# Row sums of the later modulation: four products, or a weighted sum on VectorE and one product

## The chip, the cores and the metric

The kernel runs on one core of a Trainium2 chip. The metric is the device time of one execution in microseconds (us). Before the change it is 3398.08 us, the median of 3 runs (3396.28 to 3401.31).

## What is computed

The reference is one layer of a decoder trunk for 1,024 tokens of width 2,048. Two sub-layers (a token mixer with four head groups, and a mixture of experts) are each modulated by shift, scale and gate vectors. All six vectors come from one product of the conditioning vector c with a matrix of 2,048 rows and 12,288 columns:

```python
mod = (jax.nn.silu(c) @ w_ada[l] + b_ada[l]).astype(F32)
sh1, sc1, gt1, sh2, sc2, gt2 = jnp.split(mod, 6, axis=-1)
h = ada_input(x, sh1, sc1)
p = h @ w_in[l]
...
x = layer_norm(ALPHA * x + (1.0 + gt1)[:, None, :] * y_mix, ln_g[l, 0], ln_b[l, 0])
h = ada_input(x, sh2, sc2)
```

The change touches only how the last four of these vectors (gt1, sh2, sc2, gt2: 8,192 columns) are computed.

## The kernel before

**Stages.** Up to about 55 us the kernel normalizes tokens and begins the first two vectors. From there to about 2,000 us it runs the input projection, the four mixers and the output projection; then routing and the experts follow, to the end at about 3,400 us.

**The order on TensorE.** In the middle stage two streams share TensorE. The mixers (RWKV, attention, S5) are written out by hand; their products depend on VectorE and ScalarE. The fills are the projections: `fills` runs over units of columns, and `unit` over 16 row tiles, with three products per tile pair (`mm3`). Wherever a mixer would wait, it calls `hop(us)`, and `pump` takes fills until their estimated cost covers that time: 0.64 for each `mm3`, 0.9 for each modulation step (`modstep`, line 618). In this stage every TensorE instruction is kept in the order of the program text (`pinned`, line 191). The other engines' orders, and that of the DMA queue on SyncE (SP), are set by the compiler's scheduler.

**Weights of the fills.** A row tile is loaded to `wraw` (four buffers), rounded by ScalarE to `whi` (line 327), and the rest is taken by VectorE to `wlo` (line 328); there are three buffers of each pair.

**The modulation steps.** `mod_parts` (line 577) is a generator with 64 steps: 16 groups `ci` of 512 columns, and in each four steps `q` of four row tiles. It is advanced once for every four row tiles of a unit (line 397). A step takes four tiles of 128 rows and 512 columns, loaded by line 587 into `mw` buffers, of which there are six (`mt`, line 221); `conv` (line 919) takes three of the same six each time. For each tile `w` four products follow (line 601), one for each 128 columns: the stationary operand is the column of silu(c) for that row tile, repeated over 32 columns, and the output is a strip of 32 partitions of `pq`, a part of the PSUM tile `rwS`. The four tiles accumulate in `pq`. After the first step of a group VectorE copies `pq` to `mdacc` (line 605), after the next two it adds (line 607), and in the last (q = 3) the bias row is added by a product with a row of ones (line 603), VectorE makes the sum (line 610), and four small DMAs write it out. Then the loads of the next step are issued (line 615). The trace counts each f32 product as two records, so a step is 32 records of weight loads and 32 of products, and the bias is 8 of each.

**The triangular solve.** `rw_core` (line 720) has a loop of 31 steps in which VectorE multiplies and reduces (lines 788 and 789); its result goes to DRAM and comes back before the next mixer products, 32 by 32 in shape (line 822).

Of the kernel before, what the change touches and what calls it, by code (L numbers as in the profile page):

```python
# [15 lines left out]
ALU = mybir.AluOpType  # L16
# [7 lines left out]
KT = D // 128  # L24
# [144 lines left out]
class K:  # L169
# [407 lines left out]
    def mod_parts(s):  # L577


        nc, io = s.nc, s.io  # L580
        jobs = [(ci, q) for ci in range(KT) for q in range(4)]

        def load(ci, q):
            ws = []
            for k in range(4 * q, 4 * q + 4):
                ws.append(s.mt())
                nc.sync.dma_start(ws[-1], io["w_ada"][128 * (KT * ci + k):128 * (KT * ci + k) + 128])
            if q == 3:
                ws.append(s.ev())
                nc.sync.dma_start(ws[-1][0:1], io["b_ada"][0:1, 2 * D + 512 * ci:2 * D + 512 * ci + 512])  # L590
            return ws

        ws = load(*jobs[0])
        yield
        pq, pm = s.rwS[:, 128:256], s.mdacc
        for i, (ci, q) in enumerate(jobs):
            for x, w in enumerate(ws):
                k = 4 * q + x
                for j in range(4):
                    if k < KT:  # L600
                        s.mm(pq[32 * j:32 * j + 32], s.cs[:, k:k + 1].to_broadcast([128, 32]), w[:, 128 * j:128 * j + 128], start=x == 0, stop=x == 3 and q < 3)
                    else:
                        s.mm(pq[32 * j:32 * j + 32], s.c["ones"][0:1, 0:32], w[0:1, 128 * j:128 * j + 128], start=False, stop=True)
            if q == 0:
                nc.vector.tensor_copy(pm, pq)
            elif q < 3:
                nc.vector.tensor_add(pm, pm, pq)
            else:
                t = ws[4][:, 0:128]
                nc.vector.scalar_tensor_tensor(t, pm, 0.0 if ci // 4 == 1 else 1.0, pq, op0=ALU.add, op1=ALU.add)  # L610
                for j in range(4):
                    nc.sync.dma_start(s.md_d[0:1, 512 * ci + 128 * j:512 * ci + 128 * j + 128], t[32 * j:32 * j + 1])
                s.nmd += 1
            if i + 1 < len(jobs):
                ws = load(*jobs[i + 1])
            yield
# [1625 lines left out]
```

## Time and profile before

| | us |
|---|---|
| median of 3 runs | 3398.08 |
| the profiled execution | 3401.34 |
| its span, first to last instruction | 3399.5 |
| TensorE products busy | 2914.0 (86%) |
| TensorE weight loads busy | 2198.7 (65%) |
| VectorE busy | 1879.4 (55%) |
| ScalarE busy | 1157.6 (34%) |

The profile page gives busy time by engine, a strip of 40 slices of about 85 us, the DMA queues, and the costliest groups of instructions. PE is TensorE's products, PEld its weight loads, DVE VectorE, ACT ScalarE, POOL GpSimd, SPq the DMA queue of SyncE. The trace can also be asked for groups of instructions by form, for who waited for whom, for busy time in windows, and for instructions in order of time. "Idle before" is the time an engine stood still just before the instructions of a group; behind "<-" stands what ended it, and "issue" means that nothing the profile shows was waited for.

### The profile page before, as it was taken

The numbers are of one execution on the slowest core, as the hardware profiler recorded it, in microseconds if no ns is written. First come the engines' busy times: TensorE is split into PE (matmuls) and PEld (weight loads), VectorE is DVE, ScalarE is ACT, GpSimd is POOL, SyncE is SP. The second block draws the span as 40 slices with busy tenths as digits, with TensorE's granted clock in tenths as the row PEclk, the third lists the DMA queues.
The fourth block names the chain that finished last, engine by engine and source line by source line (L and its number), as shares of the span: only waits on it lengthen the run. The fifth ranks groups of instructions, "written<-read, shape, count | busy, mean of one in ns | idle before, by whom it ended". The sixth has DMA issues, their size and how long they took to land. (4 is left out here: it accounts for less than half of the span.)

```text
span 3399.5 us, 58570 instructions
## 1 busy us (share of the span) xinstructions
PE 2914.0 (86%) x22607; PEld 2198.7 (65%) x22607; DVE 1879.4 (55%) x3504; ACT 1157.6 (34%) x1808; POOL 544.6 (16%) x678
## 2 busy tenths in 40 slices
PE   6889989899999999989998865798897988988950
PEld 3567666766687667667677754676665766766740
DVE  2466667774443465666646883255454454454527
ACT  4332323333322322332433441234343343343411
POOL 0057665200000000000004452000001010010002
PEclk9999999999999999999998876898998988989975
DMA  8646354654798667445347666989899799799884
GB/s 352 220 150 180 105 166 126 210 170 150 249 302 271 215 194 224 124 132 162 100 140 239 211 219 250 383 317 401 326 342 385 295 385 381 286 395 364 310 324 198
DMA packets 348842, 845.96 MB, mean 249 GB/s; under 512 B 95505, under 2 KB 175482, under 8 KB 284770
## 3 DMA queue, kind: packets, MB, share of 16 engines
q1 hardware_dynamic: 338812, 808.36, 66.2%
q0 software_dynamic: 9728, 33.61, 3.8%
q8 instruction: 184, 3.01, 0.4%
q14 instruction: 118, 0.97, 0.1%
HBM read 752.35 MB, written 108.87 MB: 253 GB/s over the span
## 5 line engine op out<-in xcount | busy, mean ns | idle before, releaser
L1893 DVE TENSOR_TENSOR partl<-raw,parth 128x1024 fp32r<-128x1024 f32 x336 | 405.3, 1222 | 319.6 <-ACT parth L1892 313.8
L328 DVE TENSOR_TENSOR wlo<-wraw,whi 128x512 fp32r<-128x512 f32 (+2 forms) x472 | 355.4, 756 | 365.4 <-ACT whi L327 352.8
L327 ACT CAST whi<-wraw 128x512 fp32r<-128x512 f32 (+2 forms) x472 | 282.4, 601 | 736.1 <-PE acc L182 590.7
L1892 ACT CAST parth<-raw 128x1024 fp32r<-128x1024 f32 x336 | 347.9, 1050 | 455.4 <-PE h L182 188.9
L182 PE MATMUL acc<-hh,whi 128*128 128x512 f32 (+1 forms) x1056 | 456.4, 437 | 11.8 <-ACT hh L354 6.4
L182 PE MATMUL acc<-hh,wlo 128*128 128x512 f32 (+1 forms) x1056 | 421.8, 401 | 21.4 <-DVE wlo L328 21.3
L182 PE MATMUL acc<-hl,whi 128*128 128x512 f32 (+1 forms) x1056 | 421.9, 400 | 0.0
L182 PE MATMUL acc<-wlo,hh 128*128 128x512 f32 x640 | 263.1, 411 | 23.1 <-DVE wlo L328 20.2
L182 PE MATMUL acc<-whi,hh 128*128 128x512 f32 x640 | 264.2, 432 | 21.7 <-DVE ev L1534 16.0
L182 PE MATMUL h<-partl,xh 128*128 128x512 f32 x608 | 259.0, 426 | 17.3 <-DVE partl L1893 17.1
L182 PE MATMUL h<-parth,xh 128*128 128x512 f32 x608 | 243.0, 420 | 24.9 <-ACT parth L1892 24.5
L182 PEld LDWEIGHTS acc<-hh,whi 128*128 128x128 f32 (+1 forms) x1056 | 203.2, 193 | 87.6 <-issue 33.1
L182 PE MATMUL acc<-whi,hl 128*128 128x512 f32 x640 | 259.5, 405 | 0.0
L182 PEld LDWEIGHTS acc<-hh,wlo 128*128 128x128 f32 (+1 forms) x1056 | 201.9, 191 | 73.5 <-DVE wlo L328 26.2
L182 PE MATMUL h<-parth,xl 128*128 128x512 f32 x608 | 248.4, 408 | 0.0
L182 PEld LDWEIGHTS acc<-hl,whi 128*128 128x128 f32 (+1 forms) x1056 | 202.6, 192 | 46.8 <-issue 10.2
L182 PE MATMUL h<-raw,x 128*32 128x128 f32 x4608 | 169.2, 286 | 25.5 <-DMA raw<-in_moe_w 21.8
L1564 POOL MEMSET pre<- 128x516 int32 x1 | 0.5, 527 | 1084.5 <-DMA r_d<-ev 1084.5
L182 PEld LDWEIGHTS h<-raw,x 128*32 128x32 f32 x4608 | 130.8, 114 | 64.3 <-issue 33.6
L182 PEld LDWEIGHTS acc<-whi,hh 128*128 128x128 f32 x640 | 124.8, 197 | 66.0 <-issue 16.9
L182 PEld LDWEIGHTS acc<-wlo,hh 128*128 128x128 f32 x640 | 126.1, 197 | 56.9 <-DVE wlo L328 28.3
L182 PEld LDWEIGHTS h<-partl,xh 128*128 128x128 f32 x608 | 121.0, 199 | 64.3 <-DVE partl L1893 31.9
(448 smaller groups left out, 4761.3 us busy)
## 6 DMA issues: line engine op xcount, KB each, us to landing
raw<-in_moe_w SPq DMA_DIRECT2D x384, 1024.0 KB
mw<-in_w_ada SPq DMA_DIRECT2D x256, 256.0 KB
wraw<-in_w_in SPq DMA_DIRECT2D x240, 256.0 KB
wraw<-in_w_out SPq DMA_DIRECT2D x160, 256.0 KB
wa<-in_wa SPq DMA_DIRECT2D x32, 1024.0 KB
pT_d<-ev SPq DMA_DIRECT2D x62, 256.0 KB
t<-s_tab SPq DMA_DIRECT2D x24, 512.0 KB
s_tab<-mw SPq DMA_DIRECT2D x32, 256.0 KB
```

Of the source, the lines that this page charges most:

```text
L182: return s.pinned(s.nc.tensor.matmul(*a, **k))
L327: s.nc.scalar.copy(v(hi), v(raw))
L328: s.nc.vector.tensor_sub(v(lo), v(raw), v(hi).bitcast(F32))
L1564: nc.gpsimd.memset(pre.bitcast(I32), BIG)
L1892: nc.scalar.copy(hi, x)
L1893: nc.vector.tensor_sub(lo, x, hi.bitcast(F32))
```

## The change

In the steps with odd q (1 and 3), VectorE multiplies the first tile by its column of silu(c), in place, and adds the three other tiles, each times its column. Four products of a matrix of ones (128 by 32) with that tile follow, one for each strip of 128 columns. The steps with even q stay as they are, as do the bias products, the sums in `mdacc`, the loads and the pacing value of 0.9.

```diff
@@ -594,8 +594,18 @@
         yield
         pq, pm = s.rwS[:, 128:256], s.mdacc
         for i, (ci, q) in enumerate(jobs):
+            if q % 2:
+
+                a = ws[0]
+                nc.vector.tensor_scalar(a, a, s.cs[:, 4 * q:4 * q + 1], None, op0=ALU.mult)
+                for x in range(1, 4):
+                    nc.vector.scalar_tensor_tensor(a, ws[x], s.cs[:, 4 * q + x:4 * q + x + 1], a, op0=ALU.mult, op1=ALU.add)
+                for j in range(4):
+                    s.mm(pq[32 * j:32 * j + 32], s.c["ones"][:, 0:32], a[:, 128 * j:128 * j + 128], start=True, stop=q < 3)
             for x, w in enumerate(ws):
                 k = 4 * q + x
+                if q % 2 and k < KT:
+                    continue
                 for j in range(4):
                     if k < KT:
                         s.mm(pq[32 * j:32 * j + 32], s.cs[:, k:k + 1].to_broadcast([128, 32]), w[:, 128 * j:128 * j + 128], start=x == 0, stop=x == 3 and q < 3)
```

## Rows read from the trace of the kernel before

**Rows 1.** TensorE's busy tenths in 40 slices; the steps' products, first and last start

```profile
PE   6889989899999999989998865798897988988950
...
L182 PE MATMUL rwS<-mw,cs x2048: 272/273/418, 704.1 to 1363.9; 128*32 128x128 f32 x187
```

**Rows 2.** Busy time of 704 to 1365 us (columns as the first line says)

```profile
core 0: us, PE busy (x) PEld busy (x) DVE busy (x) ACT busy (x) POOL busy (x), PEclk, DMA share, GB/s
704.00:1365.00 661.00, 639.01 (x5281) 468.62 (x5282) 340.56 (x790) 202.37 (x381) 0.10 (x1) 0.98 0.71 227
```

**Rows 3.** PE's waits, 704 to 1365 us, longest first: total, times, longest

```profile
PE rwA L182 <- ACT t L1037: 3.9, 1, 3.9
PE rwS L182 <- DMA mw<-in_w_ada: 3.8, 7, 1.3
```

**Rows 4.** Groups by form: products of the steps and of the bias

```profile
L182 PE MATMUL rwS<-mw,cs 128*32 128x128 f32 x2048 | 71.1, 276 | 4.4 <-DMA mw<-in_w_ada 3.8 <-DVE St L876 0.6
...
L182 PE MATMUL rwS<-ev,per 1*32 1x128 f32 x128 | 6.7, 280 | 0.0
```

**Rows 5.** Weight loads in order of time at a q = 3 step: start, duration

```profile
943.21 0.81 PEld L182 LDWEIGHTS rwS<-mw,cs 128*32 128x32 f32 x32
944.22 0.15 PEld L182 LDWEIGHTS rwS<-ev,per 1*32 1x32 f32 x8 [0.20 <-issue]
944.57 0.19 PEld L182 LDWEIGHTS acc<-hh,whi 128*128 128x128 f32 x1 [0.20 <-issue]
944.68 0.19 PEld L182 LDWEIGHTS acc<-hl,whi 128*128 128x128 f32 x1
944.91 0.19 PEld L182 LDWEIGHTS acc<-hh,wlo 128*128 128x128 f32 x1
```

**Rows 6.** VectorE in `conv`: shortest, median and longest duration in ns

```profile
L930 DVE TENSOR_SCALAR mw<-mw,vecs x8: 478/481/487, 550.0 to 1467.9; 128x512 f32<-128x512 f32 x8
...
L931 DVE SCALAR_TENSOR_TENSOR mw<-mw,vecs x8: 732/747/754, 551.6 to 1468.6; 128x512 f32<-128x512 f32 x8
```

**Rows 7.** The page's groups: the rounding of the fills' weights

```profile
L328 DVE TENSOR_TENSOR wlo<-wraw,whi 128x512 fp32r<-128x512 f32 (+2 forms) x472 | 355.4, 756 | 365.4 <-ACT whi L327 352.8
L327 ACT CAST whi<-wraw 128x512 fp32r<-128x512 f32 (+2 forms) x472 | 282.4, 601 | 736.1 <-PE acc L182 590.7
```

**Rows 8.** Two solves in order of time: VectorE's last reduction, then TensorE's next products

```profile
1222.26 0.42 DVE L789 TENSOR_REDUCE t<-tv 128x8 f32<-128x256 f32 x1
...
1239.99 0.69 PE L182 MATMUL rwB<-t,t 32*32 32x32 f32 x32
...
1476.73 0.42 DVE L789 TENSOR_REDUCE t<-tv 128x8 f32<-128x256 f32 x1
...
1486.58 0.90 PE L182 MATMUL rwB<-t,t 32*32 32x32 f32 x32 [4.22 <-DMA t<-xn_d]
```

**Rows 9.** Loads of tiles and the products that waited for them, in time

```profile
1235.01 0.81 SPq L587 DMA_DIRECT2D mw<-in_w_ada  x2
...
1239.39 0.42 PE L182 MATMUL rwS<-mw,cs 128*32 128x128 f32 x8 [0.35 <-DMA mw<-in_w_ada]
...
1312.85 0.33 SPq L587 DMA_DIRECT2D mw<-in_w_ada  x1
...
1315.71 0.42 PE L182 MATMUL rwS<-mw,cs 128*32 128x128 f32 x8 [0.32 <-DMA mw<-in_w_ada]
...
1330.41 0.42 PE L182 MATMUL rwS<-mw,cs 128*32 128x128 f32 x8 [0.50 <-DMA mw<-in_w_ada]
```

**Rows 10.** Waits of SP's queue and of ACT, 680 to 1370 us

```profile
SPq L587 <- PE rwS L182: 79.1, 79, 5.7
...
ACT t L1265 <- DMA t<-u_d: 23.3, 7, 4.6
```

**Rows 11.** Busy time of two short windows (columns as in rows 2)

```profile
1350.30:1353.70 3.40, 1.59 (x31) 0.70 (x30) 0.69 (x1) 0.62 (x1) 0.00 (x0) 1.00 0.85 226
1353.70:1357.10 3.40, 3.40 (x15) 2.44 (x16) 0.29 (x1) 0.00 (x0) 0.00 (x0) 0.51 0.94 285
```

## The prediction

> **What bounds the kernel now.** I read the strip of 40 slices first, to see which engine is full where the modulation steps run. The steps' products start between 704.1 and 1363.9 us, slices 9 to 16, and TensorE stands there at 9 tenths in nearly every slice [rows 1]. Next the busy time of that stretch: of 661 us TensorE's products cover 639.0, its weight loads 468.6, VectorE 340.6 (52%), ScalarE 202.4, GpSimd nothing, and the granted clock is 0.98 of full [rows 2]. A modelled busy time doesn't prove a bound, so the list of waits comes third: of what TensorE's products wait for in this stretch, the longest total is 3.9 us, in one wait, and the second is 3.8 us for the tiles `mw` of the steps themselves [rows 3]. VectorE, in turn, stands idle mostly for ScalarE's rounding, which stands idle for TensorE to free its buffers [rows 7]. So the other engines wait for TensorE, and here TensorE's own work is the time. What it saves in this stretch should shorten the kernel, since the later stages follow from the fills in order.
>
> **What is removed from TensorE.** A step is 32 records. In order of time, the weight loads of a q = 3 step begin at 943.21, those of the bias at 944.22, those of the next fill at 944.57 [rows 5]. So 32 records take 1.01 us up to the next instruction, and 8 take 0.35, with a fixed 0.20 of turnaround in both. An odd step goes from 32 records to 8 of nearly the form of the bias products: it saves 1.01 - 0.35 = 0.66 us. There are 32 odd steps of 64, so 32 x 0.66 = 21.1 us. The ends: the bare loads go from 0.81 to a quarter, 0.20, which gives 32 x 0.61 = 19.5; the groups' busy times, 71.1/64 = 1.11 and 6.7/16 = 0.42 [rows 4], give 32 x 0.69 = 22.1. I take 21.1, from the starts, since they are what the next instruction sees.
>
> **What is added to VectorE.** One multiplication by a column and three multiply-adds, each 128 by 512 in f32 from SBUF. `conv` has both in the same form: 0.481 and 0.747 us [rows 6]. A step costs 0.481 + 3 x 0.747 = 2.72 us, all 32 cost 87 us. VectorE goes from 340.6 to 428 of 661 us (65%). I cost this at nothing by itself, for two covers. First, the weights of the fills: a product of a fill starts every 0.23 us (944.68 to 944.91, [rows 5]), a pair of buffers serves 12 products, 2.8 us, and two pairs are in hand when the third is refilled: 5.5 us, less 0.60 of rounding and 0.76 of subtraction [rows 7], leaves 4.2 us, more than 2.72. Second, the mixers' own chains, which the list of waits shows to be late for little [rows 3]. If the first cover is gone, each odd step costs what goes beyond 4.2 us.
>
> The tightest chain is the triangular solve, a loop of VectorE alone: one ends at 1222.68, and TensorE takes up its result at 1239.99 without a wait, 17.3 us later. Another ends at 1477.15, and there TensorE has to wait until 1486.58, so the way through DRAM takes 9.4 us [rows 8]. The slack of the first is 17.3 - 9.4 = 7.9 us. In a unit of two column tiles a step comes after every 24 products of 0.23 us, so with its own 1.01 us they stand 6.5 us apart; the solve's 31 hops of 0.88 us cover some 28 us of fills, so two of the four steps in it are odd. With one that begins before, two or three sums fall into it, 5.4 to 8.2 us, and TensorE comes 1.3 to 2.0 us earlier: the stall is between 0 and 2.3 us. I take 1.1 us, the middle, for this one solve, and nothing for others in the stretch, which could cost as much each at the upper end.
>
> **The wait that is added.** The four products now wait for VectorE, which waits for all four tiles. Behind the products stands everything on TensorE; behind the sums stand the next `wlo` and the mixers. The loads are issued a step ahead. Two tiles were in buffers before, and the last two are issued when the step before has freed theirs. From such an issue to the products that waited for it I read 4.4 us (1235.01 to 1239.39) and 2.9 us (1312.85 to 1315.71) [rows 9]. After the last tile TensorE had only its own records to do; now up to two multiply-adds come between, 1.5 us. Most odd steps hide this: their last loads are issued about 1 us into the step before, 5.5 us or more ahead, against 3.7 us of landing (the mean of the two) and 1.5. The three that waited for a tile before, at 1239, 1315 and 1330 [rows 9], pay it: 3 x 1.5 = 4.5 us. The ends are a gain of 3.8 us, where the waits for tiles go altogether because VectorE frees three buffers of an odd step before TensorE comes to it, and a loss of 1.5 us in each of ten odd steps, 15 us.
>
> SP's queue holds the loads until TensorE frees a buffer: 79 waits, 79.1 us [rows 10]. After an odd step it waits for VectorE instead, which is earlier, and the weights of the fills queued behind come no later. The number and size of all DMAs stays. The copies and sums in `mdacc`, the bias products and the pacing value of 0.9 stay, at nothing.
>
> A wait can also cost clock. Between 1350.3 and 1353.7 TensorE waited for tiles, with weight loads busy for 0.70 of 3.40 us; in the next window the granted clock was 0.51, the 1.2 GHz level, after 1.00 before [rows 11]. A window of 3.4 us at half the clock is worth up to 1.7 us. The Trainium skill, "TensorE: Matmul & The Clock Gate", section "HAM oscillation", says that repeated waits between short bursts make every burst start at the lower clock, which would speak against a change that adds waits. By that rule the three waiting steps would cost up to 3 x 1.7 = 5 us more, and the sum would come out 5 us higher. The row agrees in kind. I leave it out of the sum, since the stretch as a whole ran at 0.98 [rows 2], and keep it for the range.
>
> **Sum.** -21.1 + 4.5 + 1.1 = -15.5 us against the profiled execution's own 3401.34, which gives 3385.8. That execution is 3.3 us above the median of 3398.08; against the median the sum is 3382.6. I say 3383. By the ends of the terms it lies from -22.1 - 3.8 (3372) to -19.5 + 4.5 + 2.3 + 5 (3390); further losses belong to the rivals.
>
> **Rivals.** What a measurement of this kernel can tell from no change is about 0.2%, 6.8 us: 3391.3 to 3404.9 counts as the same.
>
> *The time saved is waited away.* An odd step still reports 0.9 to the pacing but takes 0.66 us less, so each mixer product that stands behind it comes 0.66 us sooner and, where its operand was just in time, waits that much longer. For it: the weight loads cover only 71% of the stretch [rows 2], so TensorE may have less to gain than its products' 97% says. Against it: the mixers' operands are late in few places now [rows 3], while the same TensorE saving is made in front of all the fills. The Trainium skill, "Perfetto Trace Analysis", section "Identifying the Most-Contended Engine", says that busy matmul time is a poor measure and that of the weight loads a good one; by it TensorE isn't full here, and the time would stay at 3398. The waits in this trace don't agree so far. This decides where the added waits reach 0.66 us for each odd step; ten steps at 1.5 us and 2.3 at the solve leave -4 us, 3394, and all of it gives 3398. Together with the case that the sum is right in sign but falls short of 6.8 us, this has a chance of 0.25.
>
> *VectorE is held at the head of its queue (slower).* Its order is fixed beforehand. Where a sum was put in front of work that is ready, but its tile lands late, everything behind it waits: `wlo`, then TensorE. For it: ScalarE is held that way now, 7 times by the load of `u_d`, for 3.3 us on average and 4.6 at most [rows 10], and tiles take 2.9 to 4.4 us to land. Against it: half of a step's tiles are there long before. Price: a hold of 3.3 and 2.72 of work, less the cover of 4.2, is 1.8 us for each odd step, 58 in all; less 21 that is +37, 3435. It decides where the hold exceeds 4.2 - 2.72 + 0.66 = 2.1 us; at 2.5 us it is +11, 3409. Chance 0.20.
>
> That the change doesn't do what it says can be left out: the removed products are skipped in the program text.
>
> **How the numbers follow.** The forecast's case has 0.55: faster by over 0.2% is 0.55, the same 0.25, slower 0.20. The predicted time is the forecast's, 3383, with its own range of 3372 to 3390. The range for 8 in 10 goes down to 3370, the best ends of the terms, and up to 3410, which takes in no change and the milder half of the slower rival; some 0.1 of the chance lies above it and less below.
>
> **What would show it.** The products of the steps fall from 2,048 records to 1,024 with silu(c) and 256 with ones. VectorE shows 32 multiplications near 0.48 us and 96 multiply-adds near 0.75, 87 us more in this stretch. From the first step to the last takes some 15 us less than 660 us, and the stages behind take what they did. TensorE's waits for VectorE's sums stay near 5 us. If those waits exceed 20 us, or waits for `wlo` grow from almost nothing, a rival has it; if the stretch shortens and a later stage lengthens, the bound was elsewhere, and the sum is wrong for a reason that isn't named here.

## The result: slower by 0.9%, and the profile after

The changed kernel takes 3428.20 us (median of 4 runs, 3423.42 to 3430.94) against 3399.69 us for the kernel before beside it. The ratio is 1.0088, with an interval of 1.0069 to 1.0108. The forecast was 3383, so 45 us are missing. In the changed file the lines behind the sum stand 10 further down: the solve's pair is L798 and L799, the sum itself is L600 (the multiplication by a column) and L602 (the multiply-adds).

First the instructions of the sums, as groups by line or by form of the kernel after (count, then busy us and mean ns, then the idle time before them):

```profile
L602 DVE SCALAR_TENSOR_TENSOR mw<-mw,cs 128x512 f32<-128x512 f32 x96 | 71.9, 749 | 92.7 <-DMA mw<-in_w_ada 92.0
...
L600 DVE TENSOR_SCALAR mw<-mw,cs 128x512 f32<-128x512 f32 x32 | 15.5, 485 | 70.9 <-DMA mw<-in_w_ada 65.9 <-issue 5.1
```

```profile
L182 PE MATMUL rwS<-mw,cs 128*32 128x128 f32 x1024 | 34.6, 276 | 0.2 <-DVE mdacc L617 0.2
...
L182 PE MATMUL rwS<-mw,per 128*32 128x128 f32 x256 | 14.3, 298 | 14.0 <-DVE mw L602 13.9
```

The counts are as foreseen, 1,024 and 256 for 2,048 [rows 4], and so are the durations, 485 and 749 ns for 481 and 747 [rows 6]. What was not there before stands behind the bar: VectorE was idle for 158 us (92.0 + 65.9) just before instructions of the sum, until a row tile landed. Such a stand at the head of VectorE's queue is called a hold below. The list of waits, which is used from here on, gives 153 us for the same (89.3 + 63.8).

Next the busy time of the stretch. The steps now run from 704.7 to 1396.6 us, 692 us instead of 660. The second window is the one that answers to [rows 2], from the first step to the last:

```profile
core 0: us, PE busy (x) PEld busy (x) DVE busy (x) ACT busy (x) POOL busy (x), PEclk, DMA share, GB/s
704.00:1365.00 661.00, 611.51 (x4282) 441.26 (x4280) 389.89 (x874) 195.33 (x372) 0.10 (x1) 0.95 0.69 217
704.00:1397.00 693.00, 635.26 (x4506) 459.43 (x4504) 412.64 (x918) 201.19 (x381) 0.10 (x1) 0.95 0.69 217
```

TensorE's products are idle for 693.00 - 635.26 = 57.7 us, against 661.00 - 639.01 = 22.0 before: 36 us more. And the mean clock is 0.95 for 0.98. With only two levels, a mean of 0.95 says that about a tenth of the window ran at 1.2 GHz; added up in the two traces it is 75 us of 693, and 20 of 661 before. The busy time fell by 3.8 us where 21 were saved; the 17 between them are put down to the clock, which is an estimate: of the 55 us more at 1.2 GHz TensorE stood still through some 18, and at half speed the other 37 cost 18. So of 32 us lost, 36 are standing, some 17 are clock, and 21 are saved.

What TensorE's products wait for, in the stretch of the steps (total, times, longest):

```profile
PE rwS L182 <- DVE mw L602: 13.9, 6, 4.5
PE rwB L182 <- DMA t<-xn_d: 11.6, 2, 8.3
PE rwB L182 <- DVE t L837: 7.2, 1, 7.2
PE rwB L185 <- ACT t L1351: 4.3, 2, 3.2
```

The products of the steps waited 3.8 us for tiles before [rows 3]; those of the odd steps now wait 13.9 us for the sum. The next two rows are larger together: 18.8 us, in three waits, for the solve's result, which `xn_d` and L837 carry on; neither is in the list before. L1351 belongs to S5. The three waits for the solve in order of time:

```profile
786.41 1.73 PE L182 MATMUL rwB<-t,t 32*32 32x32 f32 x32 [7.18 <-DVE t L837]
1257.97 1.07 PE L182 MATMUL rwB<-t,t 32*32 32x32 f32 x32 [3.32 <-DMA t<-xn_d]
1391.41 1.07 PE L182 MATMUL rwB<-t,t 32*32 32x32 f32 x32 [8.26 <-DMA t<-xn_d]
```

What VectorE and SP's queue wait for in the same stretch:

```profile
DVE mw L602 <- DMA mw<-in_w_ada: 89.3, 54, 4.8
DVE mw L600 <- DMA mw<-in_w_ada: 63.8, 23, 9.0
DVE wlo L328 <- ACT whi L327: 35.4, 28, 2.5
```

```profile
SPq L587 <- DMA mw<-in_w_ada: 65.6, 45, 4.4
SPq L587 <- PE rwS L182: 45.0, 34, 6.4
SPq L587 <- DVE mw L602: 37.4, 51, 1.7
```

77 of the 128 instructions of the sums found their tile not landed. The loads waited for TensorE 34 times instead of 79 [rows 10], and 51 times for a multiply-add. One q = 3 step in order of time shows how the two hang together. First its loads on SP's queue, then its four instructions on VectorE, then TensorE:

```profile
1201.81 0.47 SPq L587 DMA_DIRECT2D mw<-in_w_ada  x1
1210.60 0.38 SPq L587 DMA_DIRECT2D mw<-in_w_ada  x1
1215.59 0.33 SPq L587 DMA_DIRECT2D mw<-in_w_ada  x1
1218.98 2.23 SPq L587 DMA_DIRECT2D mw<-in_w_ada  x5
```

```profile
1207.92 0.48 DVE L600 TENSOR_SCALAR mw<-mw,cs 128x512 f32<-128x512 f32 x1
...
1214.81 0.75 DVE L602 SCALAR_TENSOR_TENSOR mw<-mw,cs 128x512 f32<-128x512 f32 x1 [1.21 <-DMA mw<-in_w_ada]
1215.47 0.33 DVE L798 TENSOR_TENSOR tv<-t,t 128x96 f32<-128x96 f32 x1
...
1218.21 0.75 DVE L602 SCALAR_TENSOR_TENSOR mw<-mw,cs 128x512 f32<-128x512 f32 x1 [0.47 <-DMA mw<-in_w_ada]
...
1223.67 0.75 DVE L602 SCALAR_TENSOR_TENSOR mw<-mw,cs 128x512 f32<-128x512 f32 x1 [2.45 <-DMA mw<-in_w_ada]
1224.34 0.28 DVE L799 TENSOR_REDUCE t<-tv 128x8 f32<-128x128 f32 x1
```

```profile
1224.48 0.43 PE L182 MATMUL rwS<-mw,per 128*32 128x128 f32 x8 [4.54 <-DVE mw L602]
```

The third load is issued at 1215.59, when the multiply-add of the second tile ends (1214.81 + 0.75), and the fourth at 1218.98, when that of the third ends (1218.21 + 0.75). A multiply-add frees a buffer, the next load takes it, lands 2.6 to 4.7 us later, and the next multiply-add, already at the head of VectorE's queue, waits for it. Between the multiply-adds stand the instructions of the triangular solve (L798, L799), which are held as well. This solve began at 1194.12 and took 28.6 us before; now it runs from 1206.94 to 1246.87, 39.9 us. The stretch has three solves. Added up in the traces, they took 28.4, 28.6 and 32.1 us, and now take 33.5, 39.9 and 47.3. Inside the three stand 29 of the 128 operations of the sums, with 19.5 us of work and 9 us of holds, so holds are the smaller part there.

At the end of the step shown TensorE stands 4.54 us for the sum. The clock of three stretches around that wait (columns as above):

```profile
1217.10:1220.50 3.40, 2.84 (x13) 2.02 (x11) 2.83 (x9) 1.17 (x2) 0.00 (x0) 1.00 0.89 298
1220.50:1223.90 3.40, 0.00 (x0) 0.00 (x0) 0.95 (x5) 0.00 (x0) 0.00 (x0) 1.00 0.86 271
1223.90:1227.30 3.40, 2.82 (x21) 1.94 (x22) 3.23 (x9) 0.00 (x0) 0.00 (x0) 0.67 0.72 263
```

TensorE stands through the middle one, and in the next, at a mean of 0.67, part of the time is at 1.2 GHz. So this wait is paid again in clock.

### The profile page after: what moved, and what is told of

Same layout as the page of the kernel before. It is cut to its first block, busy times and chain, and to the rows that moved or that the text cites. A ratio compares the mean times of both kernels' runs of the same rounds, so it can differ in the third digit from the quotient of the medians.

```text
span 3428.7 us, 57126 instructions
## 1 busy us (share of the span) xinstructions
PE 2903.5 (85%) x21839; PEld 2185.6 (64%) x21839; DVE 1951.5 (57%) x3632; ACT 1156.6 (34%) x1808; POOL 540.4 (16%) x678
```

## The experiments

Three theories stood at the start: "hold" (VectorE stands at the head of its queue for tiles that come one by one), "work" (the 87 us of VectorE's work delay the mixers), and "latency" (TensorE waits for the end of the sum). All ratios are to the kernel before, run beside each kernel.

| run | us | ratio, interval | holds | PE waits for the sum |
|---|---|---|---|---|
| the change | 3428.20 | 1.0088 (1.0069 to 1.0108) | 153 | 13.9 |
| r1 last tile first | 3438.60 | 1.0107 (1.0090 to 1.0124) | 66 | 41.7 |
| r2 in program order | 3481.47 | 1.0231 (1.0214 to 1.0248) | 9 | 85.1 |
| r3 work alone | 3413.73 | 1.0026 (1.0013 to 1.0038) | 0 | no sum |
| r4 on GpSimd | 3467.14 | 1.0190 (1.0173 to 1.0207) | on GpSimd | 50.4 |
| r5 seven buffers | 3433.22 | 1.0087 (1.0065 to 1.0108) | 134 | 0 |
| r6 eight buffers, before | 3389.40 | 0.9960 (0.9945 to 0.9974) | 0 | no sum |
| r7 eight buffers | 3404.61 | 1.0020 (1.0005 to 1.0035) | 101 | 0 |
| r8 eight, last tile first | 3384.89 | 0.9951 (0.9929 to 0.9973) | 42 | 0 |
| r9 touches | 3430.74 | 1.0084 (1.0054 to 1.0114) | 150 | no sum |
| r10 touches, reversed | 3433.32 | 1.0101 (1.0070 to 1.0131) | 148 | no sum |
| r11 seven, last tile first | 3425.07 | 1.0061 (1.0038 to 1.0084) | 61 | 27.7 |
| r12 touches in program order | 3402.44 | 1.0023 (1.0006 to 1.0041) | 20 | no sum |
| r13 nine, last tile first | 3425.53 | 1.0087 (1.0067 to 1.0107) | 61 | 0 |
| r14 nine buffers, before | 3413.50 | 1.0044 (1.0030 to 1.0058) | 0 | no sum |
| r15 sum a step ahead | 3397.62 | 0.9982 (0.9964 to 0.9999) | 9 | 13.4 |

The last two columns are us, from the waits of VectorE and TensorE between 704 and 1450 us.

**r1, the sum begins with the last tile.**

```diff
-a = ws[0]
-nc.vector.tensor_scalar(a, a, s.cs[:, 4 * q:4 * q + 1], None, op0=ALU.mult)
-for x in range(1, 4):
+a = ws[3]
+nc.vector.tensor_scalar(a, a, s.cs[:, 4 * q + 3:4 * q + 4], None, op0=ALU.mult)
+for x in (2, 1, 0):
```

> The changed kernel, but the sum begins with the tile that is loaded last, so that VectorE cannot begin it before all four tiles have buffers. Theory 'hold' (VectorE's fixed order puts the sum early, the tiles come one after another through two spare buffers, and VectorE stands at the head of its queue for each): VectorE's waits for the tiles fall from 153 us to under 60, and the time falls by 15 us or more, to 3413 us or less. Theory 'work' (87 us of added VectorE work delays the mixers): 3420 to 3435 us, since the work is the same. Theory 'latency' (TensorE waits for each sum's end): 3428 us or more, since the sum now ends later after the last tile.

3438.60, so "hold" in its simple form and "work" missed, and "latency" fits. The holds fell as meant, but the waits moved. VectorE's and TensorE's rows:

```profile
DVE mw L600 <- DMA mw<-in_w_ada: 66.5, 26, 6.2
```

```profile
PE rwS L182 <- DVE mw L602: 41.7, 17, 8.1
```

In this order no buffer is freed before the last tile is in. The last two loads wait for the products of the step before, and behind their landing stands the whole sum, 2.7 us, instead of one multiply-add. TensorE waits 41.7 us for 13.9.

**r2, the sum at its place in program order.**

```diff
-nc.vector.tensor_scalar(a, a, s.cs[:, 4 * q:4 * q + 1], None, op0=ALU.mult)
+s.paced(nc.vector.tensor_scalar(a, a, s.cs[:, 4 * q:4 * q + 1], None, op0=ALU.mult))
```

> The changed kernel, with the first operation of each sum kept behind everything that the program text has before it on VectorE. Theory 'hold': waits for the tiles on VectorE under 60 us, TensorE's waits for the sums larger than 30 us, time between 3395 and 3415 us. Theory 'work': 3420 to 3435 us. Theory 'latency': above 3435 us.

3481.47. Almost no holds are left, and the time is the worst of all, as "latency" has it and neither of the others. TensorE's first wait, and VectorE around the longest one:

```profile
PE rwS L182 <- DVE mw L602: 85.1, 27, 9.8
```

```profile
1206.23 0.75 DVE L718 SCALAR_TENSOR_TENSOR tp<-tp,vecs 128x512 f32<-128x512 f32 x1
1206.89 0.48 DVE L600 TENSOR_SCALAR mw<-mw,cs 128x512 f32<-128x512 f32 x1
1207.41 2.33 DVE L602 SCALAR_TENSOR_TENSOR mw<-mw,cs 128x512 f32<-128x512 f32 x3
```

The last load of this step was issued at 1186.44, 20 us before. The tiles were there, and the sum stood behind a run of mixer instructions without a gap; TensorE waited 9.8 us until 1209.79. So a sum that is not put ahead of the mixers is late for TensorE, by 85 us in all; the kernel lost 79 against before.

**r3, VectorE's work alone.** All products stay, and in odd steps VectorE does four operations of the same form on a zero tile.

```diff
+a = s.dum
+s.paced(nc.vector.tensor_scalar(a, a, s.cs[:, 4 * q:4 * q + 1], None, op0=ALU.mult))
+for x in range(1, 4):
+    nc.vector.scalar_tensor_tensor(a, a, s.cs[:, 4 * q + x:4 * q + x + 1], a, op0=ALU.mult, op1=ALU.add)
```

> The kernel before, with all its products, and in each odd step the same four VectorE operations on a tile of zeros that stays in SBUF and that nothing reads; they are kept in program order. Theory 'hold': within 8 us of the kernel before (3392 to 3408 us), since nothing is waited for. Theory 'work': the loss of the change plus the TensorE time that isn't saved here, 28 + 21 = 49 us, about 3449 us.

3413.73 against 3402.58: 11 us, by its interval 4 to 13, somewhat over the 3408 of "hold" and far under the 3449 of "work". Its multiply-adds never stood (idle 1.5 us):

```profile
L601 DVE SCALAR_TENSOR_TENSOR dum<-dum,cs 128x512 f32<-128x512 f32 x96 | 71.6, 746 | 1.5
```

So 87 us on VectorE aren't free, as the prediction had them, but cost about half of what TensorE saves. In r3's trace 6 to 7 us of it stand from the first step on (the table at the end of this section), and 4.5 before the first step, where nothing was changed. And this is the price of work in program order; where the scheduler puts the change's sums, more of them fall into the solves (29 operations for r3's 21), and r3 doesn't price that.

**r4, the sum on GpSimd**, which does nothing else in this stretch.

```diff
-nc.vector.tensor_scalar(a, a, s.cs[:, 4 * q:4 * q + 1], None, op0=ALU.mult)
-for x in range(1, 4):
-    nc.vector.scalar_tensor_tensor(a, ws[x], s.cs[:, 4 * q + x:4 * q + x + 1], a, op0=ALU.mult, op1=ALU.add)
+for x in range(4):
+    nc.gpsimd.tensor_scalar(ws[x], ws[x], s.cs[:, 4 * q + x:4 * q + x + 1], None, op0=ALU.mult)
+    if x:
+        nc.gpsimd.tensor_tensor(a, a, ws[x], op=ALU.add)
```

> The changed kernel, with the sums on GpSimd, which is idle in this stretch (four multiplications and three additions for each odd step, about 10 us). Theories 'hold' and 'work': VectorE is free of it, TensorE's saving of 21 us shows, 3378 to 3392 us. Theory 'latency': a sum takes four times as long as on VectorE, so 3428 us or more.

3467.14, although VectorE has no part in the sums here. GpSimd's groups:

```profile
L601 POOL TENSOR_SCALAR mw<-mw,cs 128x512 f32<-128x512 f32 x128 | 212.2, 1663 | 417.8 <-DMA mw<-in_w_ada 356.7 <-DVE t L845 31.7 <-PE acc L182 13.8
L603 POOL TENSOR_TENSOR mw<-mw 128x512 f32<-128x512 f32 x96 | 129.2, 1346 | 6.6
```

A tile now takes 3.0 us after it has landed (1.66 + 1.35) instead of 0.75, and TensorE waits 50 us. GpSimd's own 357 us of waiting for tiles hold next to nobody: but for one short MEMSET nothing else stands on GpSimd in this stretch. This and r2 show a price of its own, as "latency" has it: TensorE's wait for the sum.

**r5 to r8, more buffers**, to have the tiles earlier. r5 is the change with `bufs=7`. For eight, the mixers' pool of 2 KB tiles gives one up; r6 does this to the kernel before, r7 to the change, r8 to the order of r1:

```diff
-return s.M.tile([128, 514], F32, name="mw", tag="mw", bufs=6)[:, 0:n]
+return s.M.tile([128, 514], F32, name="mw", tag="mw", bufs=8)[:, 0:n]
...
-s.np, s.n2, s.n4, s.n8 = 6, 9, 6, 2
+s.np, s.n2, s.n4, s.n8 = 6, 8, 6, 2
```

> The change with seven row-tile buffers instead of six, nothing else altered. 'buffers' (the loss is TensorE's idle time and the half clock behind it; both come of it that with six buffers the four tiles of an odd step cannot be in and summed a step ahead): one more tile can be ahead, so about half of the loss goes: 3400 to 3418, VectorE's holds for row tiles from 153 us to under 100, half-clock time of the stretch between the fill products that stand at 700 and 1450 before (34 us before, 75 after) under 60. 'sum' (the sum itself is too long and sits too late on VectorE, however early its tiles come): 3422 or more, and the waits of TensorE for the sum stay at 14 us or above.

> The kernel before with eight row-tile buffers; to make room the mixers' pool of 2 KB tiles has eight instead of nine. A control for the next two. Both theories: four products per step as before, loads up to a whole step earlier; TensorE waited only 3.8 us for row tiles before, so 3390 to 3405 unless the smaller pool of 2 KB tiles delays the mixers, which would show as VectorE, ScalarE or DMA waits of TensorE on mixer tiles.

> The change with eight row-tile buffers and eight 2 KB tiles, against the control beside it. 'buffers': the tiles of a step are in a whole step ahead, holds on VectorE under 50 us, waits for the sum under 5 us, half-clock time as before; the change is then worth its 21 us of products less some 10 for VectorE's work, so 5 to 20 us under the control, about 3380 to 3398. 'sum': still 15 us or more over the control, waits for the sum above 14 us.

> As the one before, with the sum beginning with the last of the four tiles, so that VectorE's queue can be held by a row tile only once in a step. 'buffers': the order no longer matters: within 8 us of the one before, under the control; waits for the sum from 41.7 us (six buffers, this order) to under 8 us. 'sum': 3425 to 3440 as with six buffers, waits for the sum above 25 us.

r5 fits neither theory: no wait for the sum is left, as "buffers" would have it, but it takes 3433.22. r6, the control, came a little under its range. r7 misses "buffers" by time (15 us above the control) and "sum" by its waits (none). r8 lies 4.5 us below the control, as "buffers" has it, but not within 8 us of r7. r7 and r8 do the same work with the same buffers, and in neither does TensorE wait for the sum; they differ in the order of the four operations, and by 20 us (14 of them, in the traces, between the first step and the mixers' last products). VectorE's holds in r5, r7 and r8:

```profile
DVE mw L600 <- DMA mw<-in_w_ada: 71.0, 26, 10.0
DVE mw L602 <- DMA mw<-in_w_ada: 62.6, 49, 3.1
```

```profile
DVE mw L600 <- DMA mw<-in_w_ada: 63.2, 24, 7.8
...
DVE mw L602 <- DMA mw<-in_w_ada: 37.4, 44, 2.6
```

```profile
DVE mw L600 <- DMA mw<-in_w_ada: 41.7, 21, 6.5
```

At the top of TensorE's list in r7 stand waits for the solve's result. In r8 those are smaller, though another mixer wait (L857, 7.2 us) is new:

```profile
PE rwB L182 <- DMA t<-xn_d: 14.3, 2, 8.3
PE rwB L182 <- DVE t L837: 5.4, 1, 5.4
```

```profile
PE rwB L182 <- DMA t<-xn_d: 8.9, 2, 5.0
```

r8 beats both kernels: 0.9951 of before. But the control r6 does nearly as well without the change (0.9960, the intervals overlap), and in both the first step already stands earlier (697.6 and 694.1 us for 704.1). So no gain of the sums is shown; that of the buffers and pools is. (r6's trace is of its longest run, 3404.08, and doesn't show where the gain lies.)

**r9 and r10, holds without work.** The kernel before, with all products; in odd steps VectorE also copies one column of each tile to a small tile that nobody reads.

```diff
+if q % 2:
+    for x in (0, 1, 2, 3):
+        nc.vector.tensor_copy(s.tch[:, x:x + 1], ws[x][:, 0:1])
```

> The kernel before with all its products and six buffers; in every second step VectorE also copies one column of each of the four row tiles, in tile order, into a small tile that nobody reads. So VectorE must wait for each tile as in the change, but has almost nothing to compute (four copies of 128x1) and TensorE waits for none of it. 'hold' (a VectorE that waits at the head of its queue for tiles that land one by one delays the mixers' chains behind it, about 20 us by the difference of the two eight-buffer kernels): 3412 to 3428, holds for row tiles over 80 us. 'work and sum only' (the loss is VectorE's 87 us of work and TensorE's waits for the sum): 3398 to 3408, whatever the holds.

> As the one before, with the last of the four tiles touched first, so that VectorE can be held once in a step and mostly when it has nothing else. 'hold': at most half of the extra time of the one before, 3400 to 3414, holds for row tiles under 70 us. 'work and sum only': the same as the one before within 4 us.

> The change with the sum beginning with the last tile, and seven row-tile buffers, no other pool changed. With six buffers this order waited 41.7 us for the sum (3438.6), with eight none (3384.9). 'hold' with 'buffers' (two separate prices: holds, which this order takes away, and waits for the sum, which buffers take away): between, 3390 to 3415, waits for the sum 5 to 20 us. If seven buffers give 3430 or more, as they did in tile order (3433), buffers and order are not two separate prices.

r9 took 3430.74, 31 us more, even over the 3428 of "hold", for 19 us of work on VectorE, no removed product and no wait for any sum. VectorE's row and its group:

```profile
DVE tch L599 <- DMA mw<-in_w_ada: 150.4, 100, 4.9
```

```profile
L599 DVE COPY tch<-mw 128x1 f32<-128x1 f32 x128 | 19.4, 152 | 152.3 <-DMA mw<-in_w_ada 152.1
```

r10 was meant to hold less and did not (148 us, 3433.32). Unlike the operations of the sum, the four copies don't depend on each other, so the order of the text ties nothing, and the run, at the time of r9, tells nothing apart. r11 lies 10 us over its range: 61 us of holds and 27.7 us of waits for the sum, one more buffer than r1 and 14 us of waits less.

**r12, the same touches without the holds.** The copies are kept at their place in program order, just ahead of the products.

```diff
-nc.vector.tensor_copy(s.tch[:, x:x + 1], ws[x][:, 0:1])
+s.paced(nc.vector.tensor_copy(s.tch[:, x:x + 1], ws[x][:, 0:1]))
```

> The kernel before with the same four copies of 128x1 in every second step, but kept on VectorE at their place in program order (just ahead of that step's products), when the tiles have landed. 'hold' (the 30 us of the touches in tile order came of VectorE standing for tiles that had not landed): holds for row tiles under 20 us and a time of 3396 to 3410. 'touch' (something else of the touches, as buffers kept longer or work on VectorE): 3420 to 3435 again.

```profile
DVE tch L599 <- DMA mw<-in_w_ada: 19.7, 16, 3.9
```

The holds fall from 150 to 20 us and the time to 3402.44, 4.5 us over before by the medians (2 to 14 by the interval) instead of 31. Nothing but VectorE's order was changed. This shows the hold as a cause by itself. But not all of the 27 us between the two traces stand where the copies do. The mixers' last products (`rwS<-t,t`, the last start) before, then the steps' and the mixers' products in r9 and in r12:

```profile
L182 PE MATMUL rwS<-t,t x256: 222/270/369, 363.2 to 1636.2; 128*64 128x64 f32 x128
```

```profile
L182 PE MATMUL rwS<-mw,cs x2048: 272/273/422, 701.1 to 1381.7; 128*32 128x128 f32 x187
L182 PE MATMUL rwS<-t,t x256: 222/270/369, 361.3 to 1656.9; 128*64 128x64 f32 x128
```

```profile
L182 PE MATMUL rwS<-mw,cs x2048: 272/273/423, 703.8 to 1372.6; 128*32 128x128 f32 x187
L182 PE MATMUL rwS<-t,t x256: 222/270/369, 361.7 to 1642.4; 128*64 128x64 f32 x128
```

From the first step to the last r9 takes 680.6 us and r12 668.8; to the mixers' last products 955.8 and 938.6. So 131 us of holds cost 12 to 17 us where they stand. Another 12 us of r9's time lie behind the mixers, where the two kernels have the same text. And of the 12 us up to the last step only some 5 are TensorE's standing; the rest is busy time, with 31 us at 1.2 GHz in r9 and 17 in r12. So in r9 about half of the hold's price goes with the clock, by this one execution of each; why the clock fell more there is not shown.

**r13 to r15, the change without either price.** r13 and r14 are the order of r8 and the kernel before with nine buffers (one more pool shortened, `s.np` from 6 to 5). r15 has eight buffers, loads two steps ahead, and the sum of an odd step in program order ahead of the even step's products:

```diff
+if q % 2 == 0:
+    total(q + 1, wn)
...
-ws = load(*jobs[i + 1])
+ws = bias(*jobs[i + 1], wn)
+if i + 2 < len(jobs):
+    wn = load(*jobs[i + 2])
```

> The change with the sum beginning with the last tile and nine row-tile buffers; the pool of 2 KB tiles has eight instead of nine, the pool of 128x576 tiles five instead of six. 'hold': holds at or under the 42 us of eight buffers, no wait for the sum, so the 21 us of products less VectorE's work remain: 5 to 15 us under the control beside it. If it is within 3 us of the control, VectorE's work eats the whole saving even without holds.

> The control: the kernel before with nine row-tile buffers and the same two smaller pools. All theories: 3385 to 3400, as with eight buffers (3389.4), or some microseconds more where the smaller pools delay a mixer.

> The change with eight row-tile buffers (2 KB tiles eight instead of nine, as in the control, 3389.4), tiles loaded two steps ahead, and the sum of an odd step kept in program order just ahead of the products of the even step before it: VectorE comes to it when the tiles are in, TensorE needs it a step later. Holds under 25 us and waits for the sum under 5 us if that works. 'two prices' (holds and waits for the sum are all that the change pays beside VectorE's work, some 11 us): 3372 to 3386, 21 less 11 under the control. 'work' (VectorE's time eats the saving without any hold): 3387 to 3400.

r13 missed, and r14 lies over its 3400. The shorter pool cost the kernel before 15 us, and the change with nine buffers had 61 us of holds, more than with eight, and lies 12 us over its control. Where the scheduler puts the sum isn't governed by the number of buffers alone. r15 came to 3397.62, in the range of "work", but it did not keep its own condition. Holds are at 9 us, yet TensorE waits four times for the sum, 13.4 us.

So none of these is the change with neither price. Against the eight-buffer control the best is -4.5 us (r8) and the others +8 (r15) and +15 (r7).

**Where the time stands.** One traced execution of each kernel, in us:

| run | first step at | from it to the last step's start | to the mixers' last products | from there to the end |
|---|---|---|---|---|
| before | 704.1 | 659.8 | 932.1 | 1763.3 |
| the change | 704.7 | 691.9 | 957.2 | 1766.8 |
| r3 | 708.6 | 665.8 | 939.0 | 1762.1 |
| r7 | 693.0 | 674.3 | 944.4 | 1763.8 |
| r8 | 694.1 | 660.4 | 930.1 | 1756.0 |
| r9 | 701.1 | 680.6 | 955.8 | 1769.3 |
| r12 | 703.8 | 668.8 | 938.6 | 1756.9 |
| r15 | 690.1 | 658.2 | 934.2 | 1772.2 |

The first and last columns differ by up to 19 and 16 us, though no step stands there (r7, r8 and r15 have other pools, too). So a few us of a whole kernel's time can't be put down to the sums without a look at where they stand. In the columns between, r8 and r15 come to within some 2 us of before: there the sums, even with two more buffers, cost what they save.

## Why the prediction was wrong

**Right: what TensorE saves.** The records and the durations hold: the products of the steps are busy for 34.6 + 14.3 = 48.9 us instead of 71.1 [rows 4], 22 less, by the prediction's third way of counting. **Right: the stages behind.** The loss is in the stretch of the steps, which is 32 us longer; 7 of that are made up by the mixers' last products, and what follows takes what it did within 4 us.

**Wrong: "The wait that is added".** This is the first of two steps that failed, with its three waiting steps of 1.5 us and a possible gain "because VectorE frees three buffers of an odd step before TensorE comes to it". It took the loads to be issued as before, two tiles ahead and two about 1 us into the step before. But the freed buffers don't bring the next step forward; in the step shown they let the tiles follow each other one by one, load, multiply-add, load, multiply-add. So 77 of the sums' 128 operations waited, 153 us in all, not three steps. On TensorE the term measures 13.9 us for the sum where 4.5 was forecast; what the holds cost through the mixers had no term in the sum.

**Wrong: "What is added to VectorE".** This is the second. The work was set at nothing with two covers; r3 puts it at some 11 us, 6 to 7 of them from the first step on. The first cover held: TensorE's waits for `wlo` did not grow. The second, the mixers' own chains, was read from the waits as they were, before 153 us of holds and 87 us of work came on top. For the solve the step named the right chain and the right way, through `xn_d`, but gave 1.1 us for one solve and nothing for others. After that one (the second of three) TensorE waited 3.3 us, with 6.7 us of sums in the solve, inside the 5.4 to 8.2 foreseen, and 5.0 of holds. After the two that were priced at nothing it waited 7.2 and 8.3 us. So 18.8 us stand where 1.1 was forecast, the largest miss among TensorE's waits.

**Wrong in size: the clock.** The text kept the clock's price, 5 us, for the range because the stretch ran at 0.98. It now runs at 0.95, by the estimate above some 17 us. The Trainium skill, "TensorE: Matmul & The Clock Gate", section "HAM oscillation", says that waits between bursts send the bursts back to the lower clock; the stretches from 1217 to 1227 agree, with 1.00 before the wait of 4.54 us and 0.67 behind it.

**The rivals.** "VectorE is held at the head of its queue" came true, with 0.20 where 0.55 went to the forecast. That holds cost time is shown by r9 and r12. Its size was near (3435 for 3428), but by luck: it ran through `wlo`, for which TensorE waits hardly at all (1.6 us), where the runs show the mixers, and its hold was 3.3 us for each odd step where the trace has 153/32 = 4.8. What spoke against it, "half of a step's tiles are there long before", was taken from the loads of before. "The time saved is waited away" isn't borne out: TensorE stands 36 us longer, which is more than it saved, and largely at waits that were not there before. By the rule named there, of the Trainium skill, "Perfetto Trace Analysis", section "Identifying the Most-Contended Engine", TensorE was not full, with its weight loads at 71%. The runs agree only so far, that TensorE's time was not what decided.

**The sum, again.** From the traces, between the first step and the marks of the table above: -21 for the products, +6 to +7 for the work (r3), +14 to +20 for 153 us of holds at 12 to 17 us per 131 (r9 less r12), +14 for waits for the sum, is +13 to +20, an estimate. Measured is +32 to the last step and +25 to the mixers' last products. So 5 to 19 us are left over. What the sum lacks is work and holds in the same solve: in r3 the three solves took 101.8 us together and in r9 97.7, for 89.1 before, and TensorE waited neither for `xn_d` nor for the copy behind it; with both in the change they took 120.7, and TensorE waited 18.8. r7, with no wait for the sum, points the same way: its terms come to -6 to -1, measured is +12 to +15, and its waits for the solve's result are 19.7. That this fills the gap is argued, not shown; no run takes the sums out of the solves alone. The clock is in each of the terms, and no run takes it out. Open too are what the sums are worth with neither price, and why nine buffers held VectorE more than eight.

## What to carry to other kernels

When work moves to an engine whose order is fixed beforehand, look up what each moved instruction waits for, and who stands behind it in that queue: a load that lands a few us late delays all of them, even if the engine has idle time to spare. Look also at which chains the added work falls into: the sums that landed in a solve were waited for, while in r3 the same 87 us cost little. Moving the instruction back in the queue exchanged the hold for a wait of the engine that needs the result (r2, 85 us); with the sum a step earlier and two more buffers (r15) 13 us of that were left. And operands that are freed one by one as they are used invite loads to come one by one too: count the buffers for all operands of one result, beside those of the step that is running.

## What was not expected

VectorE was 52% busy in this stretch [rows 2], and standing for 150 us in pieces of 1.5 us (r9, 100 waits) still made it 21 us longer: idle time of an engine in the trace is not time that it has to give. The Trainium skill, "PSUM — Partial Sum Buffer", section "Engine vs sequencer instructions", says that VectorE's queue is strictly first in, first out; the solve that waits between two multiply-adds in the trace above agrees. Two more buffers, at the cost of one 2 KB tile, made the kernel before faster by 0.4% (r6, 12 us), more than any form of the change gained over its own control (r8, 4.5 us).
